# Attention block 1: normalizing the value products in place of the probabilities

## The chip, the cores and the metric

The kernel runs on one core of a Trainium2 chip. The metric is the device time of one launch in microseconds. The engines are TensorE (PE), VectorE (DVE), ScalarE (ACT), GpSimd (POOL) and the queue that issues transfers (SyncE, SP). They run side by side, each through its own list of instructions in order, and wait for one another by semaphores.

## The reference

Two transformer blocks on 256 positions of width 1024, in float32. The change is in the attention of the first one: 256 latent queries over 512 keys (256 of a context, 256 latent). Four A heads are differential: two softmaxes with 64-wide queries and keys, one minus lambda times the other, times 128-wide values, then an RMS norm over the 128 values. Eight B heads are ordinary, 96 wide, with 64-wide values.

```python
def _diff_attend(q1, q2, k1, k2, v, lam):
    s1 = einsum('bqhd,bkhd->bhqk', q1, k1) * scale
    s2 = einsum('bqhd,bkhd->bhqk', q2, k2) * scale
    a = softmax(s1) - lam * softmax(s2)
    return einsum('bhqk,bkhe->bqhe', a, v)

def _softmax_attend(q, k, v):
    a = softmax(einsum('bqhd,bkhd->bhqk', q, k) * scale)
    return einsum('bhqk,bkhe->bqhe', a, v)

oa = rmsnorm(oa, diff_subln) * (1 - lam_init)
out = concat(oa, ob) @ w_out
```

## The kernel before

Activations lie transposed: features on the 128 partitions, 256 positions along the row. Every weight matrix comes from memory in tiles of 128x2048 (`raw`, three buffers, issued by SP), and is split by ACT (`hi`) and DVE (`lo`) into two parts. Projections multiply these in three matmuls of 128x256 per 128x128 weight tile.

The program is first recorded, then ordered by a list scheduler written into the kernel (`schedule`, line 485): it has costs for each instruction, models the PE clock and the port that DVE and POOL share, takes for each engine the instruction that can start first (the order of the program breaks ties), and assigns buffers. Tiles of a tag (`tp`, `la`, `s`, ...) in PSUM are given out in the program's order. `BUFS` (line 683) gives `tp` two banks, `s` two, `la` and `v5` one each; scores alternate over `s`, `v5`, `s`. `issue` (line 635) then emits all instructions, so every row of the profile carries its line, L666, and rows are told apart by their tiles. There `c` stands for all 256- and 512-wide work tiles, `col` for columns, `v` for the tag `v5`.

Block 1's attention works on units: `unit` (line 1252) computes the softmax of one unit and then the value product of the unit before. A unit is one A head, or a pair of B heads.

- `softA` (line 1181): for each of two query tiles of 128 and each of the two softmaxes, a score matmul into PSUM, the maximum over 512 keys (DVE), its negated scaled copy (DVE), the exponential with the sum as a by-product (ACT). Then two reciprocals, lambda multiplied into the second, the second set of probabilities scaled (128x512; DVE for query tile 0, POOL for tile 1, `POOL_A`), and one DVE instruction that scales the first set and subtracts.
- `softB` (line 1220): the same with one softmax per query tile; the probabilities are scaled by 1 / z in a 128x512 instruction (POOL for query tile 0, DVE for tile 1, `POOL_B`).
- `transposed` (line 1162): eight PE transposes of 128x128 into two `tp` banks, each copied out by ACT (128x512).
- `pvA` (line 1204), `pvB2` (line 1239): value matmuls in full fp32 into the `la` bank, four of 128x256 for an A head, eight 64 wide for a B pair. A head's product is squared, its squares summed over the partitions by a matmul with ones, and normalized. The result is split into two parts in `cat`.

Between the units lie other pieces: the projections `qa`, `vc`, `kB`, `qB`, `vB` (`ORDER`); products of the `ada` matrices with a vector (`gemv`, line 975), whose 128x1024 multiplies go to DVE or POOL, in the latter case summed by ACT; and the output projection's terms for heads that are done (`wout_part`, line 1319).

Of the kernel before, what the change touches and what calls it, by code (L numbers as in the profile page):

```python
# [15 lines left out]
OP = mybir.AluOpType  # L16
# [662 lines left out]
def _build(ctx, tc, nc, A, out):  # L679
# [33 lines left out]
    def mm(o, a, b, start, stop):  # L713
        PE.matmul(o, a, b, start=start, stop=stop)
# [441 lines left out]
    V.tensor_tensor(lam[:, 2:3], lam[:, 0:1], lam[:, 1:2], OP.subtract)  # L1156
    lam_init = 0.8 - 0.6 * math.exp(-0.3 * 0)
    V.tensor_scalar(lam[:, 2:3], lam[:, 2:3], lam_init, None, op0=OP.add)
    subln = K("subln", [128, 1])
    V.tensor_scalar(subln, col("subln"), 1.0 - lam_init, None, op0=OP.mult)  # L1160

# [17 lines left out]
    SC = ("s", "v5", "s")  # L1179

    def softA(h):
        pa = []
        for qt in range(2):
            tq = slice(128 * qt, 128 * qt + 128)
            zs = T("col", [128, 2])
            pz = []
            for z in range(2):
                mx = T("col", [128, 2])
                r = slice(64 * z, 64 * z + 64)
                s_ = PSR([128, 512], SC)  # L1190
                mm(s_, qA[h][r, tq], kA[h][r], True, True)
                V.tensor_reduce(mx[:, 0:1], s_, AX.X, OP.max)
                V.tensor_scalar(mx[:, 1:2], mx[:, 0:1], -scA, None, op0=OP.mult)
                p = c2()
                ACT.activation(p, s_, AF.Exp, bias=mx[:, 1:2], scale=scA, accum_out=zs[:, z:z + 1])
                pz.append(p)
            V.reciprocal(zs, zs)
            V.tensor_tensor(zs[:, 1:2], zs[:, 1:2], lam[:, 2:3], OP.mult)
            (G if qt in POOL_A else V).tensor_scalar(pz[1], pz[1], zs[:, 1:2], None, op0=OP.mult)
            V.scalar_tensor_tensor(pz[0], pz[0], zs[:, 0:1], pz[1], op0=OP.mult, op1=OP.subtract)  # L1200
            pa.append(pz[0])
        return pa

    def pvA(h, pa):
        aT = transposed(pa)
        o_ = PS("la", [128, 256])
        for kt in range(4):
            mm(o_, vA[h // 2][kt][:, 128 * (h % 2):128 * (h % 2) + 128], aT[kt], kt == 0, kt == 3)
        sq = c1()
        ACT.activation(sq, o_, AF.Square)  # L1210
        st = PS("tp", [128, 256])
        mm(st, ones, sq, True, True)
        rs = c1()
        rstd_of(rs, st, 128)
        V.scalar_tensor_tensor(rs, o_, subln, rs, op0=OP.mult, op1=OP.mult)
        c_ = c2(F32R)
        split(c_[:, 0:256], c_[:, 256:512], rs)
        cat.append(c_)

    def softB(h):  # L1220
        pa = []
        for qt in range(2):
            tq = slice(128 * qt, 128 * qt + 128)
            mx = T("col", [128, 4])
            s_ = PSR([128, 512], SC)
            mm(s_, qB[h][0:96, tq], kB[h][0:96], True, True)
            V.tensor_reduce(mx[:, 0:1], s_, AX.X, OP.max)
            V.tensor_scalar(mx[:, 1:2], mx[:, 0:1], -scB, None, op0=OP.mult)
            p = c2()
            ACT.activation(p, s_, AF.Exp, bias=mx[:, 1:2], scale=scB, accum_out=mx[:, 2:3])  # L1230
            V.reciprocal(mx[:, 3:4], mx[:, 2:3])
            (G if qt in POOL_B else V).tensor_scalar(p, p, mx[:, 3:4], None, op0=OP.mult)
            pa.append(p)
        return pa

    def softB2(hp):
        return softB(2 * hp), softB(2 * hp + 1)

    def pvB2(hp, pas):
        o_ = PS("la", [128, 256])  # L1240
        aT = [transposed(pa) for pa in pas]
        for kt in range(4):
            for z in range(2):
                h = 2 * hp + z
                mm2(o_[64 * z:64 * z + 64], vB[kt][:, 64 * h:64 * h + 64], aT[z][kt], kt == 0, kt == 3)
        c_ = c2(F32R)
        split(c_[:, 0:256], c_[:, 256:512], o_)
        cat.append(c_)

    pend = []  # L1250
# [723 lines left out]
```

## Time and profile before

| | |
|---|---|
| median of 3 runs | 780.84 us (778.87 to 781.52) |
| the profiled execution | 778.39 us, of which the span from the first to the last instruction is 776.6 us |
| PE | 743.9 us busy (96%) |
| PE weight loads | 675.2 us (87%) |
| DVE | 583.5 us (75%) |
| ACT | 430.8 us (55%) |
| POOL | 304.9 us (39%) |
| mean granted PE clock | 0.995 of full speed |

Matmuls are pipelined, so that a matmul's duration is longer than the distance to the next one, and PE counts as busy over short gaps. The shares are means over the whole launch; the attention of block 1 takes the stretch from about 85 to 195 us.

### The profile page before, as it was taken

To read this page: it belongs to the slowest core of one execution; us is meant where nothing else is said; L and a number is where in the kernel's file an instruction comes from. 1 tells how busy PE (TensorE), PEld (TensorE's weight loads), DVE (VectorE), ACT (ScalarE), POOL (GpSimd) and SP (SyncE) were. 2 spreads that over 40 slices of the span, in tenths; PEclk is the share of its full clock that TensorE was granted. 3 is DMA by queue.
4 is the path that set the end of the run, shared out by engine and by line. 5 is a ranking of instruction groups with operands and counts; after the bars stand their busy time and mean duration, and the time that the engine had idled before them with its cause. 6 is when DMAs were issued, how large, how long until landed. Compare 5 with 4: busy or idle time off the path is not lost.

```text
span 776.6 us, 15213 instructions
## 1 busy us (share of the span) xinstructions
PE 743.9 (96%) x5987; PEld 675.2 (87%) x5987; DVE 583.5 (75%) x1106; ACT 430.8 (55%) x786; POOL 304.9 (39%) x313
## 2 busy tenths in 40 slices
PE   5998999999999999999999997899999999999998
PEld 3877785557999999999999996498899999999997
DVE  6768787977999899888668898976488666654552
ACT  6435439887765365555554432578556666643441
POOL 0013154764041949998012175686250333310000
PEclk9999899999999999999999999999999999999999
DMA  8956633434597366554666621053364655556540
GB/s 332 364 212 229 217 132 114 177 108 176 204 270 273 110 257 230 181 201 167 214 227 214 214 84 55 1 170 157 110 208 173 213 172 212 180 208 199 203 176 14
DMA packets 33993, 142.88 MB, mean 184 GB/s; under 512 B 11777, under 2 KB 15233, under 8 KB 17794
## 3 DMA queue, kind: packets, MB, share of 16 engines
q1 hardware_dynamic: 33922, 141.91, 51.7%
q8 instruction: 47, 0.77, 0.4%
q14 instruction: 24, 0.20, 0.1%
HBM read 139.54 MB, written 1.05 MB: 181 GB/s over the span
## 4 chain that ended last, share of the span: by engine, by line
PE 86%; DVE 8%; ACT 3%; DMA 1%; issue 1%; POOL 0%; SPq 0%; DVEq 0%
PE mm L666 42%; PE s L666 32%; PE tp L666 6%; DVE c L666 5%; PE la L666 4%; PE v L666 3%; ACT c L666 2%; DVE lo L666 1%; DVE col L666 1%; DMA raw<-in_ada 1%; DMA k_X<-in_x 0%; DVE raw L666 0%; DVE k_adc L666 0%; ACT raw L666 0%; ACT hi L666 0%
## 5 line engine op out<-in xcount | busy, mean ns | idle before, releaser
L666 DVE TENSOR_TENSOR lo<-raw,hi 128x1024 fp32r<-128x1024 f32 x206 | 263.0, 1280 | 82.3 <-ACT hi L666 81.0
L666 ACT ACTIVATE hi<-raw 128x1024 fp32r<-128x1024 f32 x206 | 216.2, 1053 | 193.1 <-PE mm L666 94.3
L666 PE MATMUL mm<-xs,hi 128*128 128x256 f32 (+1 forms) x992 | 179.6, 282 | 0.6 <-ACT hi L666 0.4
L666 PEld LDWEIGHTS mm<-xs,hi 128*128 128x128 f32 x992 | 151.4, 188 | 3.2 <-issue 1.4
L666 PE MATMUL mm<-c,hi 128*128 128x256 f32 (+1 forms) x744 | 141.8, 289 | 4.6 <-DVE c L666 2.7
L666 PE MATMUL mm<-xs,lo 128*128 128x256 f32 (+1 forms) x496 | 138.5, 280 | 2.0 <-DVE lo L666 2.0
L666 PEld LDWEIGHTS mm<-c,hi 128*128 128x128 f32 x744 | 115.1, 190 | 14.3 <-issue 4.7
L666 PE MATMUL s<-xs,hi 128*128 128x256 f32 (+1 forms) x672 | 123.0, 283 | 0.0
L666 PE MATMUL s<-c,hi 128*128 128x256 f32 (+1 forms) x676 | 120.2, 278 | 0.0
L666 PE MATMUL mm<-c,lo 128*128 128x256 f32 (+1 forms) x372 | 106.4, 287 | 1.2 <-DVE lo L666 1.2
L666 PEld LDWEIGHTS s<-c,hi 128*128 128x128 f32 x676 | 103.2, 188 | 1.4 <-issue 0.4
L666 PEld LDWEIGHTS s<-xs,hi 128*128 128x128 f32 x672 | 102.9, 188 | 0.7 <-issue 0.4
L666 PEld LDWEIGHTS mm<-xs,lo 128*128 128x128 f32 x496 | 93.8, 189 | 2.8 <-DVE lo L666 2.2
L666 PE MATMUL s<-xs,lo 128*128 128x258 f32 (+1 forms) x336 | 94.1, 280 | 2.2 <-DVE lo L666 2.2
L666 PE MATMUL s<-c,lo 128*128 128x256 f32 x338 | 94.2, 279 | 0.0
L666 ACT ACTIVATE c<-c 128x256 fp32r<-128x256 f32 (+4 forms) x141 | 61.7, 448 | 57.4 <-DVE c L666 54.4
L666 POOL TENSOR_TENSOR raw<-raw,k_crow 128x1024 f32<-128x1024 f32 x18 | 48.0, 2668 | 111.7 <-DMA raw<-in_ada 100.2
L666 DVE TENSOR_TENSOR c<-c,c 128x256 fp32r<-128x256 f32 (+2 forms) x115 | 65.0, 577 | 20.1 <-POOL c L666 15.7
L666 POOL TENSOR_TENSOR c<-c 128x256 f32<-128x256 f32 x40 | 41.7, 1042 | 89.2 <-ACT c L666 79.0
L666 PEld LDWEIGHTS mm<-c,lo 128*128 128x128 f32 x372 | 70.7, 191 | 3.0 <-DVE lo L666 1.6
L666 PEld LDWEIGHTS s<-xs,lo 128*128 128x128 f32 x336 | 63.8, 190 | 2.9 <-DVE lo L666 2.6
L666 PEld LDWEIGHTS s<-c,lo 128*128 128x128 f32 x338 | 63.5, 188 | 0.3
(251 smaller groups left out, 1119.4 us busy)
## 6 DMA issues: line engine op xcount, KB each, us to landing
raw<-in_wseq SPq DMA_DIRECT2D x102, 1024.0 KB, 4.8
raw<-in_ada SPq DMA_DIRECT2D x20, 1024.0 KB, 4.9
tab<-in_ada SPq DMA_DIRECT2D x4, 1024.0 KB, 7.4
c<-in_w SPq DMA_DIRECT2D x8, 256.0 KB, 4.6
k_X<-in_x SPq DMA_DIRECT2D x4, 256.0 KB, 4.8
raw<-in_wseq SPq DMA_DIRECT2D x2, 512.0 KB, 8.0
tab<-in_ctx SPq DMA_DIRECT2D x4, 256.0 KB, 10.6
out<-c SPq DMA_DIRECT2D x7, 128.0 KB, 2.4
```

The source lines that it names most:

```text
L666: getattr(self.real[o.eng], o.fn)(*[val(x) for x in o.args], **{k: val(x) for k, x in o.kw.items()})
```

## The change

The probabilities stay as the exponentials leave them. For A heads, with z0 and z1 the sums of the two softmaxes, the difference is formed as p0 - (lambda z0 / z1) p1 in one instruction, and the factor 1 / z0 of each query is left for the output. For B heads 1 / z is left for the output. Since queries lie along the row in the output, each 1 / z column is spread over the partitions: a matmul takes the column, broadcast to 128 (or 64) columns, as its stationary operand and the identity as the moving one, into a new `tp` tile, and ACT copies that to the work tile `rb`. The value product is multiplied by it (DVE, into `rb`), and what follows reads `rb`.

```diff
--- before.py
+++ after.py
@@ -1156,6 +1156,7 @@
     V.tensor_tensor(lam[:, 2:3], lam[:, 0:1], lam[:, 1:2], OP.subtract)
     lam_init = 0.8 - 0.6 * math.exp(-0.3 * 0)
     V.tensor_scalar(lam[:, 2:3], lam[:, 2:3], lam_init, None, op0=OP.add)
+    V.tensor_scalar(lam[:, 3:4], lam[:, 2:3], -1.0, None, op0=OP.mult)
     subln = K("subln", [128, 1])
     V.tensor_scalar(subln, col("subln"), 1.0 - lam_init, None, op0=OP.mult)
 
@@ -1179,10 +1180,10 @@
     SC = ("s", "v5", "s")
 
     def softA(h):
-        pa = []
+        pa, rz = [], T("col", [128, 2])
         for qt in range(2):
             tq = slice(128 * qt, 128 * qt + 128)
-            zs = T("col", [128, 2])
+            zs = T("col", [128, 4])
             pz = []
             for z in range(2):
                 mx = T("col", [128, 2])
@@ -1194,57 +1195,74 @@
                 p = c2()
                 ACT.activation(p, s_, AF.Exp, bias=mx[:, 1:2], scale=scA, accum_out=zs[:, z:z + 1])
                 pz.append(p)
-            V.reciprocal(zs, zs)
-            V.tensor_tensor(zs[:, 1:2], zs[:, 1:2], lam[:, 2:3], OP.mult)
-            (G if qt in POOL_A else V).tensor_scalar(pz[1], pz[1], zs[:, 1:2], None, op0=OP.mult)
-            V.scalar_tensor_tensor(pz[0], pz[0], zs[:, 0:1], pz[1], op0=OP.mult, op1=OP.subtract)
+
+            V.reciprocal(zs[:, 2:3], zs[:, 1:2])
+            V.reciprocal(rz[:, qt:qt + 1], zs[:, 0:1])
+            V.scalar_tensor_tensor(zs[:, 3:4], zs[:, 2:3], lam[:, 3:4], zs[:, 0:1], op0=OP.mult, op1=OP.mult)
+            V.scalar_tensor_tensor(pz[0], pz[1], zs[:, 3:4], pz[0], op0=OP.mult, op1=OP.add)
             pa.append(pz[0])
-        return pa
-
-    def pvA(h, pa):
+        return pa, rz
+
+    def pvA(h, pr):
+        pa, rz = pr
         aT = transposed(pa)
+
+        rr = PS("tp", [128, 256])
+        for qt in range(2):
+            mm2(rr[:, 128 * qt:128 * qt + 128], rz[:, qt:qt + 1].to_broadcast([128, 128]), ident, True, True)
+        rb = c1()
+        ACT.activation(rb, rr, AF.Copy)
         o_ = PS("la", [128, 256])
         for kt in range(4):
             mm(o_, vA[h // 2][kt][:, 128 * (h % 2):128 * (h % 2) + 128], aT[kt], kt == 0, kt == 3)
+        V.tensor_tensor(rb, o_, rb, OP.mult)
         sq = c1()
-        ACT.activation(sq, o_, AF.Square)
+        ACT.activation(sq, rb, AF.Square)
         st = PS("tp", [128, 256])
         mm(st, ones, sq, True, True)
         rs = c1()
         rstd_of(rs, st, 128)
-        V.scalar_tensor_tensor(rs, o_, subln, rs, op0=OP.mult, op1=OP.mult)
+        V.scalar_tensor_tensor(rs, rb, subln, rs, op0=OP.mult, op1=OP.mult)
         c_ = c2(F32R)
         split(c_[:, 0:256], c_[:, 256:512], rs)
         cat.append(c_)
 
     def softB(h):
         pa = []
+        rz = T("col", [128, 4])
         for qt in range(2):
             tq = slice(128 * qt, 128 * qt + 128)
-            mx = T("col", [128, 4])
+            mx = T("col", [128, 2])
             s_ = PSR([128, 512], SC)
             mm(s_, qB[h][0:96, tq], kB[h][0:96], True, True)
             V.tensor_reduce(mx[:, 0:1], s_, AX.X, OP.max)
             V.tensor_scalar(mx[:, 1:2], mx[:, 0:1], -scB, None, op0=OP.mult)
             p = c2()
-            ACT.activation(p, s_, AF.Exp, bias=mx[:, 1:2], scale=scB, accum_out=mx[:, 2:3])
-            V.reciprocal(mx[:, 3:4], mx[:, 2:3])
-            (G if qt in POOL_B else V).tensor_scalar(p, p, mx[:, 3:4], None, op0=OP.mult)
+            ACT.activation(p, s_, AF.Exp, bias=mx[:, 1:2], scale=scB, accum_out=rz[:, qt:qt + 1])
             pa.append(p)
-        return pa
+        V.reciprocal(rz[:, 2:4], rz[:, 0:2])
+        return pa, rz
 
     def softB2(hp):
         return softB(2 * hp), softB(2 * hp + 1)
 
     def pvB2(hp, pas):
         o_ = PS("la", [128, 256])
-        aT = [transposed(pa) for pa in pas]
+        aT = [transposed(pa) for pa, _ in pas]
+
+        rr = PS("tp", [128, 256])
+        for qt in range(2):
+            for z in range(2):
+                mm2(rr[64 * z:64 * z + 64, 128 * qt:128 * qt + 128], pas[z][1][:, 2 + qt:3 + qt].to_broadcast([128, 64]), ident, True, True)
+        rb = c1()
+        ACT.activation(rb, rr, AF.Copy)
         for kt in range(4):
             for z in range(2):
                 h = 2 * hp + z
                 mm2(o_[64 * z:64 * z + 64], vB[kt][:, 64 * h:64 * h + 64], aT[z][kt], kt == 0, kt == 3)
+        V.tensor_tensor(rb, o_, rb, OP.mult)
         c_ = c2(F32R)
-        split(c_[:, 0:256], c_[:, 256:512], o_)
+        split(c_[:, 0:256], c_[:, 256:512], rb)
         cat.append(c_)
 
     pend = []
```

## Rows read from the trace of the kernel before

**Rows 1.** Busy time of each engine in stretches (us, instructions in brackets), granted clock, DMA share
```profile
core 0: us, PE busy (x) PEld busy (x) DVE busy (x) ACT busy (x) POOL busy (x), PEclk, DMA share, GB/s
85.00:93.80 8.80, 7.54 (x27) 4.22 (x25) 5.56 (x11) 6.97 (x17) 0.00 (x0) 0.78 0.65 238
...
179.40:195.00 15.60, 15.56 (x123) 12.84 (x124) 11.86 (x16) 11.53 (x27) 5.34 (x3) 1.00 0.65 243
...
113.50:179.40 65.90, 60.28 (x288) 37.51 (x287) 52.54 (x125) 56.73 (x134) 39.54 (x22) 1.00 0.39 134
```

**Rows 2.** Chain that ended last, shares by engine and group, 113.5 to 179.4 us
```profile
by line: DVE c L666 22.6%; ACT c L666 15.3%; PE s L666 11.3%; DVE col L666 10.5%; PE la L666 10.0%; PE mm L666 6.4%; PE tp L666 5.5%; PE v L666 4.6%; DVE k_adc L666 3.3%; ACT raw L666 3.1%; DVE lo L666 2.6%; POOL c L666 2.4%; DVE raw L666 1
```

**Rows 3.** The same chain in order of time: start us, us, what
```profile
129.65 1.57 POOL c L666
...
131.24 2.86 DVE c L666
...
161.20 0.47 DVE c L666 x2
...
163.98 2.92 DVE c L666 x2
...
173.42 1.63 DVE c L666
```

**Rows 4.** ACT's groups, 113.5 to 179.4 us: busy us, mean ns, idle before, releasers
```profile
L666 ACT ACTIVATE c<-s,col 128x512 f32<-128x512 f32 x18 | 12.4, 692 | 4.2 <-DVE col L666 4.2
L666 ACT ACTIVATE c<-tp 128x512 f32<-128x512 f32 x18 | 10.2, 596 | 2.5 <-PE tp L666 2.4
...
L666 ACT ACTIVATE c<-c 128x256 fp32r<-128x256 f32 x4 | 1.7, 419 | 1.6 <-DVE c L666 1.6
...
L666 ACT ACTIVATE c<-la 128x256 fp32r<-128x256 f32 x2 | 0.8, 377 | 0.2 <-PE la L666 0.2
```

**Rows 5.** POOL's groups, 85 to 195 us
```profile
L666 POOL TENSOR_TENSOR raw<-raw,k_crow 128x1024 f32<-128x1024 f32 x12 | 30.0, 2508 | 11.8 <-DMA raw<-in_ada 11.8
L666 POOL TENSOR_SCALAR c<-c,col 128x512 f32<-128x512 f32 x12 | 20.5, 1712 | 18.6 <-PE la L666 9.2 <-DVE col L666 7.3 <-PE mm L666 2.0
```

**Rows 6.** DVE's groups, 85 to 195 us
```profile
L666 DVE TENSOR_SCALAR c<-c,col 128x512 f32<-128x512 f32 x12 | 13.1, 1102 | 0.1
...
L666 DVE TENSOR_TENSOR c<-la,c 128x256 fp32r<-128x256 f32 x4 | 1.7, 415 | 0.5 <-ACT c L666 0.5
```

**Rows 7.** Instructions on the one-column tiles (col): count, ns min/median/max, first and last start
```profile
L666 DVE TENSOR_REDUCE col<-s x21: 662/680/692, 86.9 to 175.8; 128x1 f32<-128x512 f32 x21
...
L666 DVE TENSOR_SCALAR c<-c,col x12: 472/487/2662, 97.5 to 182.6; 128x512 f32<-128x512 f32 x12
...
L666 DVE SCALAR_TENSOR_TENSOR c<-c,col,c x8: 729/750/2857, 98.3 to 152.4; 128x512 f32<-128x512 f32 x8
```

**Rows 8.** POOL's instructions in order of time: start us, us
```profile
99.36 1.59 POOL L666 TENSOR_SCALAR c<-c,col 128x512 f32<-128x512 f32 x1 [0.80 <-DVE col L666]
...
164.26 2.35 POOL L666 TENSOR_TENSOR raw<-raw,k_crow 128x1024 f32<-128x1024 f32 x1 [4.07 <-DMA raw<-in_ada]
```

**Rows 9.** DVE's instructions in order of time
```profile
100.34 1.22 DVE L666 TENSOR_TENSOR lo<-raw,hi 128x1024 fp32r<-128x1024 f32 x1
...
164.24 2.66 DVE L666 TENSOR_SCALAR c<-c,col 128x512 f32<-128x512 f32 x1
```

**Rows 10.** ACT's instructions in order of time
```profile
167.00 0.69 ACT L666 ACTIVATE c<-s,col 128x512 f32<-128x512 f32 x1 [2.08 <-DVE col L666]
...
175.88 0.69 ACT L666 ACTIVATE c<-s,col 128x512 f32<-128x512 f32 x1 [1.00 <-DVE col L666]
```

**Rows 11.** The chain's PE pieces: two value products and a set of transposes
```profile
156.01 1.73 PE la L666 x8
...
182.75 1.88 PE la L666 x16
...
185.30 0.87 PE tp L666 x8
```

## The prediction

> **What bounds the kernel now.** I read the table of stretches first, to find the stage the edit touches and what its engines have to spare [rows 1]. The reader is to see three stretches. Between 85 and 93.8 us the granted clock averages 0.78 of full speed: part of it runs at the lower level, 1.2 GHz. From 113.5 to 179.4 us comes most of the softmax and value work of the eight units of heads (four A heads, four pairs of B heads); the clock is full, ACT is busy 56.7 us of 65.9, DVE 52.5, POOL 39.5. From 179.4 us on PE is busy 15.56 us of 15.60: the output projection fills it, and the rest of the kernel follows without a gap.
>
> Then the chain that ended last, for the middle stretch [rows 2]. DVE rows hold the largest shares (DVE c 22.6%, DVE col 10.5%), ACT c 15.3%; the PE groups listed sum to 37.8%. So most of this stage is latency of the softmax, and time saved here reaches the end, since PE's dense work behind it only waits to start. Before 113.5 us the first A head runs beside the qa and vc projections; there I expect nothing.
>
> The chain in order of time [rows 3] shows single pieces that belong to the scaling: a POOL scaling (1.57 us at 129.65), the DVE subtraction behind it that took 2.86 us, and DVE scalings at 161.20 (0.47), 163.98 (2.92) and 173.42 (1.63). ACT's groups [rows 4] show 4.2 us of idle before the exponentials that wait for DVE's maxima, and 2.5 us before the copies of transposed probabilities. POOL and DVE groups [rows 5, 6] give the scaling's totals.
>
> **What is removed.** Twelve POOL scalings, 20.5 us busy [rows 5], and twelve DVE scalings, 13.1 us [rows 6]. An undisturbed one on DVE takes 0.49 us (the median), the longest 2.66 [rows 7]; so 13.1 - 12 x 0.49 = 7.2 us of DVE's total is time blocked. What blocks it is seen in the instructions in order of time: the scaling at 164.24 ran 2.66 us beside the POOL multiply of an ada matrix at 164.26, which took 2.35 [rows 8, 9]. These multiplies stay (12 of them, 30.0 us [rows 5]), so the blocking goes only with the blocked operation. The maxima queued behind that scaling, for which ACT waited 2.08 us, read one PSUM tile, and no such reduction took more than 0.69 us [rows 7], so they should now run early; the same wait was 1.00 us at 175.88 [rows 10].
>
> On the chain the removed pieces are 1.57 (POOL), 0.47, 2.92 - 0.42 = 2.5 (a split subtraction of about 0.42 us shares that piece) and 1.63, and the excess of the subtraction at 131.24 over its median, 2.86 - 0.75 = 2.1 [rows 3, 7]. Sum 8.3 us. The last is unsure: the subtraction stays, and can be blocked by a multiply elsewhere.
>
> **What is added.** Small DVE columns: A gets one more one-column instruction per query tile (8), B loses one per head (8); they cancel.
>
> DVE: one 128x256 multiply with one PSUM operand in each of 8 units; its nearest row is the split's subtraction, 0.42 us [rows 6]: 3.3 us in all. B's four split subtractions now read two SBUF operands, so a POOL multiply can block them, up to 2.66 us; what waits for them is only the output projection, which has other heads' terms to do. I take nothing, and keep one such block in the range.
>
> ACT: one 128x256 copy from PSUM per unit at 0.38 us [rows 4], 3.0 us; B's split copies and A's squares now read SBUF, 0.42 instead of 0.38 [rows 4], 0.3 us more. Six units (A0 to A3, B0, B1) end within the middle stretch: 6 x 0.38 + 0.2 = 2.5 us there.
>
> PE: the trace has no full fp32 matmul of a broadcast column with 128 columns. A head's four value matmuls of 256 columns appear as eight instructions in 1.73 us, 0.216 each; a pair's eight matmuls, 64 wide, as sixteen in 1.88 us, 0.118 each [rows 11]. Half the columns, half the time: A 2 x 2 x 0.108 = 0.43 us, B 4 x 2 x 0.059 = 0.47 us. Lower end: one pass, like eight transposes in 0.87 us [rows 11], so 0.22 and 0.22 (two abreast); upper end: no time saved by the shorter stream, 0.87 and 0.94. I take the halved value, since the length halved is the only difference to the nearest row. In the middle stretch PE waits anyway. B2 and B3 end in the dense stretch, where nothing covers it: 2 x 0.47 = 0.9 us on the path (0.4 to 1.9).
>
> The two-bank tag for transposes takes one more tile per unit, held until ACT's copy, so the value matmuls get a copy and the results a multiply more of latency. In return, A's single value bank comes free after one multiply, not after the norm; I price that at nothing to 1 us and take nothing.
>
> **The sum, reckoned twice.** By the chain: if none of the additions lies on it, -8.3 + 0.9 = -7.4 us; if all lie on it for six units, each 0.43 (PE) + 0.38 (ACT) + 0.42 (DVE) = 1.23, +7.4: 0.0. Middle -3.7. By ACT, which is 86% busy and takes the chain over when DVE is relieved: idle before exponentials 4.2 us goes, of the 2.5 us before transposed copies half (they wait for scaled probabilities, but for PE too), so -5.4 + 2.5 + 0.9 = -2.0 us. Both limits act at once, so I take the mean, -2.8 us. The profiled execution took 778.39 us (span 776.6, the rest around it): 775.6. The three runs shown have a median 2.45 us above it, 780.84; from that, **778.0 us**. A measurement of this kernel can tell about 0.3% from no change, 2.3 us; the forecast lies just beyond.
>
> **Against the Trainium skill.** During the POOL scaling at 99.36 (1.59 us) DVE subtracted two SBUF operands at 100.34 in 1.22 us, undisturbed; only the two-operand multiplies of POOL show DVE instructions stretched to their end [rows 8, 9]. The Trainium skill, "SBUF — State Buffer", section "Who interferes with whom", says otherwise: a DVE instruction with two SBUF inputs, or in a two-port mode, shares an exclusive lock with any GpSimd instruction that reads SBUF, and the second fully blocks. By that rule the twelve POOL scalings block DVE as well, their removal gives more, and the sum would be that of the first rival below, -5.8 us, in place of -2.8 by the rows. The rows here don't bear the rule out for the scaling, and do for the multiply; I go by them.
>
> **Rivals.**
> *Deeper relief (chance 0.13).* DVE is freed not only of its own scalings but of hindrance by the 20.5 us of POOL scalings [rows 5], and ACT runs without gaps. ACT's idle in the middle stretch, 65.9 - 56.7 = 9.2 us, is the ceiling: -9.2 + 2.5 + 0.9 = -5.8 us, 775.0. For: DVE's 7.2 us of blocking. Against: ACT also waits for PE, and the subtraction at 100.34. This is what the rule of "SBUF — State Buffer" in the Trainium skill would bring.
> *Hidden (0.31).* Only the waits at 167.00 and 175.88 go (3.1 us), and ACT's 2.5 and PE's 0.9 return: +0.3 us; with half a us to two more from the transposes, about -1: 779.8, within 0.3%. For: from 125 to 143 us ACT is already almost always busy. Against: the DVE pieces on the chain.
> *ACT becomes the bound, slower (0.17).* The exponentials wait for PE's scores as before, and each added copy delays the next exponential: 3.3 us of ACT and 0.9 of PE uncovered, with one of ACT's waits saved: +4.2 - 1.0 = +3.2 us, 784.0. It decides if less than about 1 us of ACT's 9.2 us idle disappears.
> *Another order, slower (0.05).* The scheduler in the kernel orders all engines anew; a stall like that at 85 us could put PE at 1.2 GHz once more. There 8.8 us at 0.78 lost 8.8 x 0.22 = 1.9 us and PE idled 8.80 - 7.54 = 1.3 [rows 1]: +3.2 us, 784.0.
> That the scaling isn't removed cannot be: the code has none left.
>
> **Chances.** The forecast itself (2.4 to 5 us faster) gets 0.34. Faster by over 0.3%: 0.34 + 0.13 = 0.47; within: 0.31; slower: 0.17 + 0.05 = 0.22. Range, 772.5 to 784: below, the chain with nothing added back (-7.4, 773.4) and up to 1 us from the value bank; above, the two slower cases. The forecast's own range is 775.5 to 779.
>
> **What would show it.** In the changed profile: no POOL or DVE 128x512 scaling from 85 to 190 us, POOL down by about 20 us, DVE by about 10 (13.1 less 3.3), ACT up by about 3; idle before the exponentials well under 4.2 us; the start of PE's dense stretch some 3.7 us earlier than 179.4 (2.8 and the 0.9 that it gives back); the new matmuls at about 0.1 us an instruction. I am wrong if ACT's waits for DVE return at other places (multiplies of POOL that block the subtractions of A or weight splits in front of maxima), if transposes wait for their bank, or if weights arrive too late for the earlier dense stretch.

## The result, and the profile after

The changed kernel is slower, by 0.8%: 784.72 us in the median of 12 runs (781.44 to 790.82), against 778.68 us of 12 runs of the kernel before; the ratio is 1.0079, with a 95% interval of 1.006 to 1.0099. The profiled execution has a span of 783.5 us; that of the kernel before had 776.6.

The scalings are gone, as the groups of the changed kernel from 85 to 195 us show (busy us, mean ns, idle before, releasers):

```profile
L666 POOL TENSOR_TENSOR raw<-raw,k_crow 128x1024 f32<-128x1024 f32 x12 | 31.2, 2607 | 28.5 <-DMA raw<-in_ada 27.8 <-ACT c L666 0.8
...
L666 DVE SCALAR_TENSOR_TENSOR c<-c,k_subln,c 128x256 f32<-128x256 f32 x4 | 5.3, 1328 | 0.0
...
L666 DVE TENSOR_TENSOR c<-la,c 128x256 f32<-128x256 f32 x8 | 3.4, 423 | 9.0 <-PE la L666 8.9
...
L666 ACT ACTIVATE c<-tp 128x256 f32<-128x256 f32 x8 | 3.2, 401 | 1.4 <-PE tp L666 1.4
...
L666 PE MATMUL tp<-k_cst,col 128*64 128x128 f32 x32 | 2.8, 284 | 0.0
...
L666 PE MATMUL tp<-k_cst,col 128*128 128x128 f32 x16 | 2.7, 294 | 3.9 <-ACT c L666 3.9
```

No scaling on POOL or DVE is left, where [rows 5, 6] had twelve each. The additions are there as well: eight DVE multiplies of 0.42 us, eight ACT copies of 0.40, and 48 PE instructions for the spreading, 5.5 us busy (durations of matmuls that follow one another overlap). The ACT groups of the middle stretch answer to [rows 4]:

```profile
L666 ACT ACTIVATE c<-s,col 128x512 f32<-128x512 f32 x15 | 10.5, 701 | 1.3 <-DVE col L666 1.2
L666 ACT ACTIVATE c<-tp 128x512 f32<-128x512 f32 x16 | 9.1, 603 | 0.5 <-PE tp L666 0.5
```

The waits that the scalings caused shrank as forecast: 4.2 us to 1.3 before these exponentials, 2.5 to 0.5 before the copies (for 15 and 16 instructions in the stretch, where it held 18 of each). So the relief took place. But part of ACT's waiting for DVE came back elsewhere. All of it in the middle stretch (us in total, times, longest), in the kernel before and then in the changed one:

```profile
ACT c L666 <- DVE col L666: 4.2, 4, 2.1
...
ACT c L666 <- DVE c L666: 2.0, 3, 1.3
```

```profile
ACT c L666 <- DVE c L666: 2.9, 4, 1.6
ACT c L666 <- DVE col L666: 2.2, 2, 1.2
```

That is 5.1 us in place of 6.2. The stretches of the changed kernel, in the columns of [rows 1], tell why the relief is worth so little:

```profile
core 0: us, PE busy (x) PEld busy (x) DVE busy (x) ACT busy (x) POOL busy (x), PEclk, DMA share, GB/s
113.50:179.40 65.90, 61.24 (x325) 41.19 (x326) 47.88 (x112) 58.38 (x140) 25.19 (x13) 1.00 0.41 142
179.40:195.00 15.60, 15.60 (x125) 12.29 (x124) 7.92 (x17) 10.64 (x25) 0.00 (x0) 1.00 0.56 202
```

In the middle stretch DVE has 4.7 us less to do and POOL 14.4 us less, but PE is busy 61.24 us of 65.90, and was busy 60.28 before [rows 1]. PE had 5.6 us to give in this stretch, and has 4.7 now. The chain that ended last says the same. Its shares from 113.5 to 179.4 us, and some of its pieces in order of time (start us, us, what):

```profile
by line: PE mm L666 19.5%; PE la L666 16.6%; PE tp L666 16.1%; PE s L666 15.3%; DVE c L666 11.8%; PE v L666 8.8%; ACT c L666 7.4%; issue 2.7%; DVE col L666 2.0%
...
124.54 2.39 DVE c L666 x2
...
127.09 1.27 ACT c L666 x3
...
137.00 2.62 DVE c L666 x2
...
152.86 0.45 PE tp L666 x4
...
162.95 0.59 PE tp L666 x8
...
167.82 2.33 DVE c L666
```

The PE groups sum to 76.3%, against 37.8% in [rows 2]. PE's last wait ends, and its dense stretch starts, at 171.63 us instead of 179.4, almost eight us earlier, yet the residual update behind it comes at the same time, 196.46 us against 196.56: the work that PE did beside the DVE chain before now stands in a row, with the spreading matmuls in it (0.45 us of an A head at 152.86, 0.59 of a B pair at 162.95).

Three DVE pieces are left on the chain, and they are no scalings. The instructions of the changed kernel in order of time, DVE's and then POOL's (start us, us, and what each is):

```profile
124.54 2.06 DVE L666 SCALAR_TENSOR_TENSOR c<-c,k_subln,c 128x256 f32<-128x256 f32 x1
...
137.00 2.29 DVE L666 SCALAR_TENSOR_TENSOR c<-c,k_subln,c 128x256 f32<-128x256 f32 x1
...
167.82 2.33 DVE L666 TENSOR_TENSOR c<-c,c 128x256 fp32r<-128x256 f32 x1
...
123.93 2.39 POOL L666 TENSOR_TENSOR raw<-raw,k_crow 128x1024 f32<-128x1024 f32 x1
...
136.62 2.39 POOL L666 TENSOR_TENSOR raw<-raw,k_crow 128x1024 f32<-128x1024 f32 x1
...
164.61 7.77 POOL L666 TENSOR_TENSOR raw<-raw,k_crow 128x1024 f32<-128x1024 f32 x3 [1.23 <-DMA raw<-in_ada]
```

Each runs beside a POOL multiply of an ada matrix. The first two end 0.28 us after it (at 126.60 and 139.29 us, the multiplies at 126.32 and 139.01), as the scaling at 164.24 did in [rows 8, 9]; the third lies within a row of three multiplies. The norm of an A head read its product from PSUM and took 0.46 to 0.48 us in the kernel before, as here:

```profile
149.05 0.47 DVE L666 SCALAR_TENSOR_TENSOR c<-la,k_subln,c 128x256 f32<-128x256 f32 x1
```

Now that the product lies in the work tile `rb`, this instruction reads two SBUF operands and takes 1.33 us in the mean. The Trainium skill, "SBUF — State Buffer", section "Who interferes with whom", has DVE instructions with two SBUF inputs contend with GpSimd instructions that read SBUF. For the multiplies the trace agrees (2.06 to 2.33 us instead of 0.42 to 0.48).

PE pays for these three blocks. From 113.5 us to the residual update it waits three times, each time for ACT's work behind one of them (the wait stands in brackets):

```profile
128.41 0.71 PE L666 MATMUL tp<-k_cst,col 128*128 128x128 f32 x4 [1.17 <-ACT c L666]
...
141.10 0.71 PE L666 MATMUL tp<-k_cst,col 128*128 128x128 f32 x4 [2.78 <-ACT c L666]
...
171.63 0.66 PE L666 MATMUL tp<-k_cst,c 128*128 128x128 f32 x4 [0.69 <-ACT c L666]
```

The sum is 4.64 us, all but 0.02 of PE's idle time in the middle stretch. So the waits that the scalings made went, and others came in their place.

So the attention doesn't gain. Where does the loss come from? First the stretches of the kernel before that [rows 1] don't have, up to the residual update at 196.56 us and in two later stages (columns as above):

```profile
85.00:100.00 15.00, 13.74 (x68) 10.42 (x67) 10.27 (x26) 9.44 (x22) 1.53 (x2) 0.77 0.55 205
100.00:196.56 96.56, 90.43 (x522) 63.37 (x522) 77.79 (x152) 71.29 (x167) 52.95 (x28) 1.00 0.43 151
...
265.00:280.00 15.00, 15.00 (x128) 14.94 (x127) 14.76 (x20) 7.54 (x12) 14.61 (x12) 1.00 0.39 141
475.00:500.00 25.00, 19.55 (x135) 13.26 (x136) 23.09 (x106) 9.26 (x40) 15.55 (x24) 1.00 0.13 43
```

The same of the changed kernel, and its first 20 us:

```profile
0.00:20.00 20.00, 10.91 (x55) 6.24 (x56) 13.17 (x77) 11.84 (x19) 1.45 (x7) 0.91 0.91 327
85.00:100.00 15.00, 13.74 (x93) 11.26 (x92) 13.06 (x35) 9.51 (x23) 1.92 (x3) 1.00 0.65 232
100.00:196.46 96.46, 91.35 (x553) 65.62 (x553) 68.86 (x144) 74.49 (x176) 33.16 (x15) 1.00 0.46 162
265.00:280.00 15.00, 12.42 (x90) 12.01 (x89) 12.57 (x18) 4.01 (x7) 14.61 (x12) 0.89 0.41 141
475.00:500.00 25.00, 20.85 (x162) 16.19 (x163) 19.46 (x83) 8.17 (x33) 11.33 (x17) 0.80 0.13 43
```

Up to the residual update four amounts add up to the -0.1 us. The changed execution was 1.7 us late at the first scores (its clock was 0.91 in the first 20 us). The kernel before lost 15 x (1 - 0.77) = 3.45 us to the clock from 85 to 100 us, the changed one nothing. PE's idle time fell from 6.13 to 5.11 us. What is left, -0.1 - 1.7 + 3.45 + 1.0 = 2.6 us, is put down to added PE work. So the attention itself costs some 1.6 us, which the better clock of this one execution hides. The rest comes later, in code that the diff doesn't touch: 3.2 us by 405 us, 6.9 at 536 us and from there to the end. There the changed execution shows PE idle 2.58 us from 265 to 280 us where it wasn't before, and granted clocks of 0.89 and 0.80 where it was 1.00 before.

### The profile page after: what moved, and what is told of

Same layout as the page of the kernel before. It is cut to its first block, busy times and chain, and to the rows that moved or that the text cites. A ratio compares the mean times of both kernels' runs of the same rounds, so it can differ in the third digit from the quotient of the medians.

```text
span 783.5 us, 15286 instructions
## 1 busy us (share of the span) xinstructions
PE 751.2 (96%) x6035; PEld 682.6 (87%) x6035; DVE 571.5 (73%) x1103; ACT 434.5 (55%) x794; POOL 285.5 (36%) x301
## 4 chain that ended last, share of the span: by engine, by line
PE 89%; DVE 6%; DMA 2%; ACT 1%; issue 1%; SPq 0%; POOL 0%; DVEq 0%; POOLq 0%
PE mm L666 43%; PE s L666 32%; PE tp L666 7%; PE la L666 4%; DVE c L666 4%; PE v L666 3%; DVE lo L666 1%; DMA raw<-in_wseq 1%; ACT c L666 1%; DMA raw<-in_ada 1%; DVE col L666 0%; DVE raw L666 0%; SPq L666 0%; ACT hi L666 0%; POOL k_crow L666 0%
## 5 line engine op out<-in xcount | busy, mean ns | idle before, releaser
L666 PE MATMUL mm<-xs,hi 128*128 128x256 f32 (+1 forms) x992 | 181.7, 284 | 0.2 <-ACT c L666 0.2
L666 PEld LDWEIGHTS mm<-xs,hi 128*128 128x128 f32 x992 | 153.7, 191 | 2.5 <-issue 1.4
L666 PE MATMUL mm<-xs,lo 128*128 128x256 f32 (+1 forms) x496 | 140.2, 283 | 2.5 <-DVE lo L666 2.5
L666 ACT ACTIVATE c<-c 128x256 fp32r<-128x256 f32 (+4 forms) x149 | 65.2, 448 | 60.6 <-DVE c L666 57.5
L666 DVE TENSOR_TENSOR c<-c,c 128x256 fp32r<-128x256 f32 (+2 forms) x119 | 67.8, 579 | 18.8 <-POOL c L666 15.7
```

Source lines behind the costliest of these rows:

```text
L666: getattr(self.real[o.eng], o.fn)(*[val(x) for x in o.args], **{k: val(x) for k, x in o.kw.items()})
```

## The experiments

The diff's edit was taken apart in two ways. The scheduler draws the order of all engines in one go, so a change in the attention also changes the order of all later work. In most experiments the later order is pinned: for every instruction recorded after the attention (from the residual update on) the kernel first plans another variant, and each engine then takes these instructions in that plan's order. The order within the attention is not pinned (but for part of it in e3): each variant of the attention brings its own.

```diff
+            if PLAN:
+                plan = record(sp, pp, nc, A, out, PLAN)
+                plan.prepare()
+                for i in plan.schedule():
+                    o = plan.ops[i]
+                    if o.key and (PIN == "all" or o.key[1]):
+                        rec.pin.setdefault(o.eng, []).append(o.key)
...
-                for pr, i in sorted(h)[:60]:
+                q = self.pin.get(e, ())
+                for pr, i in [x for x in sorted(h)[:60] if ops[x[1]].key not in self.pinned or ops[x[1]].key == q[0]]:
```

The runs of one kernel scatter by up to 1.5%, in step with the granted clock: over 295 runs of all kernels, one slope for all, 0.01 of mean clock goes with 6.0 us of span. The last column moves each kernel's mean span to full clock with that slope (standard error 0.1 to 0.5 us; the kernel before 773.1 in 117 runs: 773.4 beside e1 to e4, 772.8 beside e5 to e8, 773.1 beside e9 to e12, 773.3 beside e13 to e15). It parts work and order from the falls of the clock; differences below about 0.8 us between two variants are within its error.

| kernel | median us | before, us | ratio, 95% interval | at full clock, us |
|---|---|---|---|---|
| changed | 784.72 | 778.68 | 1.0079 [1.006, 1.0099] | 777.7 |
| e1 new attention, old late order | 782.01 | 779.19 | 1.0027 [0.9997, 1.0056] | 775.3 |
| e2 old attention, new late order | 782.51 | 779.19 | 1.0036 [1.0013, 1.006] | 775.6 |
| e3 new attention, all else in old order | 787.81 | 779.19 | 1.0098 [1.0061, 1.0135] | 781.0 |
| e4 as e1, product kept in PSUM | 783.69 | 779.19 | 1.0059 [1.0033, 1.0086] | 777.7 |
| e5 as e1, no spreading on PE | 779.37 | 778.75 | 1.0020 [0.9995, 1.0045] | 773.6 |
| e6 A heads folded, B old, old late order | 777.95 | 778.75 | 0.9996 [0.9971, 1.0021] | 772.7 |
| e7 A heads as changed, B old | 781.12 | 778.75 | 1.0019 [0.9995, 1.0042] | 773.4 |
| e8 B heads as changed, A old | 778.72 | 778.75 | 1.0010 [0.9981, 1.004] | 774.0 |
| e9 before, late order drawn anew (+2%) | 787.32 | 778.43 | 1.0107 [1.0073, 1.0141] | 777.0 |
| e10 before, late order drawn anew (-2%) | 784.46 | 778.43 | 1.0054 [1.0024, 1.0084] | 775.5 |
| e11 as e6, spreading in one pass | 775.63 | 778.43 | 0.9976 [0.9945, 1.0007] | 770.8 |
| e12 as e1, spreading done twice | 782.83 | 778.43 | 1.0051 [1.0025, 1.0077] | 777.6 |
| e13 the kernel of e11 again | 776.91 | 777.84 | 0.9982 [0.9958, 1.0006] | 771.0 |
| e14 as e11, all orders free | 781.15 | 777.84 | 1.0033 [1.0007, 1.0059] | 774.0 |
| e15 changed, late order drawn anew | 788.56 | 777.84 | 1.0129 [1.0083, 1.0175] | 779.3 |

### Attention or order: e1 to e4

**e1**: the changed attention, the later instructions pinned to the order of the kernel before (`RUN, PLAN, PIN = "AB", "-", "late"`).

> The changed attention, but everything recorded after it (from the residual update on) is put on each engine in the order that the scheduler gave it in the kernel before. In the two profiles the first feed-forward result comes at 212.8 us before and 212.7 us after, and the 6.9 us of the longer span build up behind that point (3.2 us by the end of the first feed-forward, 6.9 us by the gated linear unit). Theory of the order (the loss is made by the new order of unchanged work): within about 1.5 us of the kernel before, 0 to -2 likelier than a loss. Rival, the stage itself (attention's own new work costs the time and the later delay is only its consequence): 5 us or more slower, like the changed kernel. Rival, the clock (stalls that were there already now meet a fall of the granted clock by their timing): somewhere between, with the falls at other places than in the changed kernel's profile.

**e2**: the old attention, the later instructions in the order of the changed kernel (`"-", "AB", "late"`).

> The attention of the kernel before, with its scalings, but everything recorded after it in the order that the scheduler gave it in the changed kernel. Theory of the order: 4 to 7 us slower than the kernel before, though not one instruction is new. The stage itself: within 1.5 us of the kernel before.

**e3**: as e1, and the work between the units of attention pinned to its old order too (`PIN = "all"`).

> The changed attention, and all other instructions, those interleaved with the attention too (projections, weight splits, products of the ada matrices, transfers), in the order of the kernel before; only the attention's own instructions are placed freely between them. Theory of the order: 0 to 3 us faster than the kernel before, since the scalings are gone and nothing else moved. The stage itself: slower by 2 us or more, since the order of before was made for the scalings.

**e4**: as e1, with the product left in PSUM:

```diff
-        V.tensor_tensor(rb, o_, rb, OP.mult)
+        V.tensor_tensor(o_, o_, rb, OP.mult)
+        rb = o_
```

> As e1, but the product of value result and 1/z is written in place into the la bank, and what follows reads it there, as before the change. In the changed profile the norm's last instruction of two A heads takes 2.06 and 2.29 us where it took 0.47 before, and two split subtractions take 1.95 and 2.33 us, each beside a POOL multiply: they now read two operands from SBUF. If that blocking costs time: 1.5 to 4 us faster than e1, and no such instruction over 0.6 us. If it is hidden: within 1 us of e1.

The loss divides in two, and neither theory has it all. The attention alone costs 775.3 - 773.1 = 2.2 us at full clock, the later order alone 2.5; together 4.7, and the changed kernel lies 4.6 above the kernel before. (e1's interval for itself just includes no change. Counted from the kernel before that ran beside them, the two are 2.0 and 2.2.) In e1 the clock from 85 to 100 us is the same as before, so its stretches compare directly:

```profile
85.00:100.00 15.00, 13.74 (x68) 10.43 (x67) 10.35 (x28) 9.46 (x21) 0.75 (x1) 0.77 0.53 201
100.00:197.62 97.62, 92.50 (x564) 67.00 (x564) 66.56 (x147) 74.28 (x175) 34.91 (x16) 1.00 0.46 160
```

PE is busy 2.07 us longer than in the kernel before (92.50 against 90.43) and idle 1.01 us less (5.12 against 6.13): 1.06 us later at the residual update, and this with DVE 11 us less busy. That is half of the 2 us; where the other half comes about, behind the residual update and with the old order held, was not looked into.

e3 is the slowest of the four: with the work between the units held in its old order too, the time is 7.9 us longer at full clock, 5.7 more than in e1, from which only this order differs. So an order within the attention can cost more than the whole edit; e3 says nothing on the later order alone. e4 came out as neither of its expectations, slower than e1. It took the second SBUF operand from the norm and the splits, and a block then met another instruction that reads two SBUF operands, as its instructions in order of time show, DVE's and then POOL's:

```profile
162.06 1.68 DVE L683 TENSOR_TENSOR c<-c,c 128x256 fp32r<-128x256 f32 x1
...
163.72 3.31 DVE L683 TENSOR_TENSOR lo<-raw,hi 128x1024 fp32r<-128x1024 f32 x1
...
158.65 10.62 POOL L683 TENSOR_TENSOR raw<-raw,k_crow 128x1024 f32<-128x1024 f32 x4 [16.93 <-DMA raw<-in_ada]
```

A weight split took 3.31 us beside four POOL multiplies in a row, and PE idled 6.0 us from 100 us to the residual update. That e4 is 2.4 us worse than e1 may come from the single value bank, held until the norm; no run tested that.

### Which part of the attention: e5 to e8

**e5**: as e1, without the spreading matmuls.

```diff
-        rr = PS("tp", [128, 256])
...
-        ACT.activation(rb, rr, AF.Copy)
+        ACT.activation(rb, aT[0], AF.Copy)
```

> The new attention with the order of e1, without the matmuls that spread 1 / z: ACT copies a tile of transposed probabilities in place of the spread factors, and the value product is multiplied by that, so the factors 1 / z are left out; ACT and DVE do as much as in e1. Theory that PE is the bound of the whole attention stage: in e1 the spreading matmuls took 5.4 us of PE's busy time from 85 to 200 us, and the chain from 113 to 198 us was almost all PE; without them the attention gives back 3 to 5 us, and the time is about 778 us, 4 us under e1 (782.0) and 1 us under the kernel before (779.2). Rival, blocked DVE instructions: the chain of e1 holds three pieces of 2.3 to 2.6 us of DVE instructions beside POOL multiplies, which stay: 781 to 783 us. Rival, ACT's added copies: these stay too: 781 to 783 us.

**e6**: only the A heads, with z0 taken out by the norm.

```diff
-            V.reciprocal(rz[:, qt:qt + 1], zs[:, 0:1])
+            V.scalar_tensor_tensor(rz[:, qt:qt + 1], zs[:, 0:1], 128 * EPS, zs[:, 0:1], op0=OP.mult, op1=OP.mult)
...
-        mm(st, ones, sq, True, True)
+        mm2(st, ones, sq, True, False)
+        for qt in range(2):
+            mm2(st[:, 128 * qt:128 * qt + 128], rz[:, qt:qt + 1].to_broadcast([128, 128]), ident, False, True)
```

> Only the A heads are changed, and in another way: the value product keeps its factor z0, and the norm takes it out, since the mean square of the scaled product plus epsilon equals (mean square + epsilon z0 squared) / z0 squared. So only epsilon z0 squared is spread by the matmuls, added into the norm's sum in PSUM; there is no ACT copy and no DVE multiply, and the norm's last instruction reads PSUM as in the kernel before. B heads and the late order as before. Theory that PE is the bound: four units of spreading remain, about 2.7 us of PE, against the gain from the A heads' scalings; near the kernel before, 778.5 to 781 us. Theory of the blocked DVE instructions: the two blocks of the A heads' norm that stand in the chain of e1 are gone, and the A heads' scalings with them: 775 to 777.5 us.

**e7** and **e8**: one kind of head as in the changed kernel, the other as before (`RUN = "A"`, `"B"`).

> The A heads as in the changed kernel, the B heads and the late order as before. PE is the bound: half of e1's loss, 780 to 781.5 us. Blocked DVE instructions: two of the three blocks in the chain of e1 belong to the A heads' norm, so most of the loss or more, 782 to 784 us. Latency and banks (the extra tile for transposes): about half, as PE.

> The B heads as in the changed kernel, the A heads and the late order as before. PE is the bound: half of e1's loss, 780 to 781.5 us. Blocked DVE instructions: one block of three, against eight scalings on DVE and eight on POOL that go: 778 to 780 us.

e5 came out between the theories: 779.37 us, where PE's theory had 778 and its rivals 781 to 783. At full clock it is 1.7 us faster than e1 (773.6 against 775.3), or 1.2 if each is counted from the kernel before that ran beside it (0.8 above 772.8, 2.0 above 773.4). So the spreading matmuls carry more than half of e1's loss; but without them the attention is only back near the kernel before. The copies, the multiplies and the blocks were left, and PE idled 6.1 us from 100 us to the residual update (95.82 - 89.70), as much as before: the relief of the scalings by itself, with these left, gained PE nothing. Counted in the same way the A heads alone lose 0.6 us (e7) and the B heads alone 1.3 (e8), each with an error of about 0.35. The theory of the blocked instructions wanted most of the loss with the A heads, and the runs speak against that; half and half, as PE's theory wanted, is within the error.

e6 came out between its two expectations as well, 777.95 us, and by its ratio at the kernel before. There the norm reads PSUM again and the copies and multiplies are gone; PE's idle time fell to 2.7 us (98.94 - 96.22). So what PE waited for can be removed, but with four units of spreading the time stays the same. Whether the spreading is what takes the gain, the next runs ask.

### The dose on PE: e11 to e13

**e11**: as e6, with the spreading in fp32r.

```diff
+        rz = T("col", [128, 2], F32R)
+        identr = K("identr", [128, 128], F32R)
...
-            mm2(st[:, 128 * qt:128 * qt + 128], rz[:, qt:qt + 1].to_broadcast([128, 128]), ident, False, True)
+            mm2(st[:, 128 * qt:128 * qt + 128], rz[:, qt:qt + 1].to_broadcast([128, 128]), identr, False, True)
```

> As e6 (A heads changed, the factor folded into the norm's epsilon, B heads and late order as before), with the spreading matmuls in fp32r, one pass in place of two. Theory that PE is the bound of the stage: in e6 PE's idle time from 100 us to the residual update fell to 2.7 us from 6.1, and the four units of spreading took about as much back; with half of that gone, about 1 us faster than e6, 776.5 to 777.5 us. Rival, that the stage's time hangs on DVE and ACT: as e6, 778 us.

**e12**: as e1, each spreading matmul issued twice.

```diff
-        for qt in range(2):
+        for qt in (0, 1, 0, 1):
```

> e1 with every spreading matmul done twice (the second overwrites the first with the same values). Theory that PE is the bound: again what the first set cost, 1 to 2.7 us over e1 (0.27% over the kernel before): 0.4% to 0.65% over the kernel before, 782 to 784.5 us. Rival, that PE has idle time to hide it: as e1.

**e13**: e11 again.

> The kernel of e11 once more, since its interval (0.9945 to 1.0007) just reaches one. If PE's relief in the attention is real: 0.25% to 0.4% faster than the kernel before. If e11's median was a lucky draw of the clock: within 0.1%.

Doubled, the spreading costs 2.3 us more at full clock (777.6 against 775.3), 0.29 us for each of the eight units; leaving it out had saved 1.2 to 1.7. PE has no time to hide it, as its theory wanted. With the cheaper spreading the A heads' part turns into a gain: e11 and e13 have ratios of 0.9976 and 0.9982. Their mean is 0.9979, with a half width of sqrt(0.0031^2 + 0.0024^2) / 2 = 0.0020: faster than the kernel before by 0.2%, with the bound of the interval at nothing; at full clock 2.2 us. e11 and e13 are 1.9 and 1.7 us faster than e6, from which they differ in half of the spreading of four units; at 0.29 us a unit that would be 0.6 us. The rest may lie in the order within the attention, which e11 has drawn anew as well; no run parts the two. The stretches of e11:

```profile
85.00:100.00 15.00, 13.74 (x94) 11.26 (x93) 13.06 (x33) 10.07 (x22) 3.56 (x3) 1.00 0.58 209
100.00:191.52 91.52, 88.59 (x505) 61.96 (x505) 68.17 (x151) 70.31 (x166) 45.49 (x23) 1.00 0.46 162
...
475.00:500.00 25.00, 21.68 (x119) 14.82 (x118) 19.32 (x98) 9.36 (x40) 16.03 (x25) 0.80 0.00 1
```

The residual update comes at 191.52 us, 5.04 before that of the kernel before. Of this 3.45 us is the clock from 85 to 100 us, which stayed full; PE's idle time is 2.93 us instead of 6.13, a gain of 3.2, and the remaining 1.6 (88.59 - 90.43 + 3.45) is PE's added work, with what moved across the ends of the stretch.

The stage can be read from one profile of each variant in the same way, from the first score matmul to the residual update, less the time that the granted clock withheld. It takes 107.4 us in the kernel before, and 107.4 to 107.8 with the old attention in e2, e9 and e10. With the new one it takes 107.9 us without the spreading (e5), 108.6 with it (e1) and 110.5 with it doubled (e12). With the A heads alone folded it takes 106.5 (e6), 105.7 (e11) and 104.9 (e13). So within each group more work on PE goes with a longer stage, by smaller steps than in the times at full clock. One kind of head alone takes 107.6 (e7) and 107.1 us (e8), which does not add up to e1's 1.2.

### Any new order: e9, e10, e14, e15

**e9** and **e10**: the kernel before, with another cost of DVE in the scheduler for the later instructions alone (1.02 and 0.98).

```diff
+        if self.late and eng == "V":
+            o.dur *= 1.02
```

> The computation of the kernel before, all of it, with the old attention; only the scheduler's cost of a DVE instruction is 2% higher for everything recorded after the attention (from the residual update on), so that only the order of the later work is drawn again. Theory that any new order of the later work costs what e2 showed, because the order of the kernel before is a good one of many: 1 to 4 us slower than the kernel before. Rival, that e2's order is bad for a reason that lies in the changed attention (its later or earlier end): no difference, within 1 us.

> As e9, with the cost 2% lower. The same two theories: 1 to 4 us slower than the kernel before, or within 1 us of it. If one of the two is slower and the other not, the cost of an order is scattered, and e2's 2 to 3 us is a draw from that scatter.

**e14**: e11 with nothing pinned. **e15**: the changed kernel with the edit of e9.

> The attention of e11, with all orders left to the scheduler. Theory that a new order of the later work costs 2 us and more whatever the attention: 0.1% to 0.8% slower than the kernel before, 2 to 8 us slower than e11. Rival, that the changed kernel's later order is bad for what its attention does: as e11.

> The changed kernel, with the scheduler's cost of a DVE instruction 2% higher for everything recorded after the attention. Theory that the order is a draw: another time than the changed kernel's (0.79% over the kernel before), by 1 us or more to either side, and still over the kernel before, since its attention alone costs 0.27% (e1).

A new order of the later work costs 2.4 to 3.9 us at full clock with the old attention, untouched (e2, e9, e10), 3.0 to 3.2 with that of e11 (e14 against e13 and e11), though e14's attention stage, 104.1 us, is no longer than theirs; and the changed kernel drawn once more is another 1.6 us slower. (By medians, falls of the clock included, e9 and e10 are 8.9 and 6.0 us slower, more than the 1 to 4 that were expected.) All five new orders are worse than the one that the kernel before has. Part of what differs is seen in PE's waits for weight splits (`lo`) from 213 to 345 us (us in total, times, longest), in the kernel before, the changed kernel and e9:

```profile
PE s L666 <- DVE lo L666: 2.2, 2, 1.2
```

```profile
PE s L666 <- DVE lo L666: 3.3, 2, 2.1
```

```profile
PE s L685 <- DVE lo L685: 6.0, 2, 4.1
```

The same row has 2.5 us in e10, 4.3 in e14 and 3.9 in e15, and 2.2 in e11, which keeps the old order. PE waits for a weight split that stands in DVE's queue behind other pieces. In e9 it is seen around the longest wait, in order of time, DVE's instructions and then POOL's and PE's:

```profile
277.66 2.27 DVE L685 SCALAR_TENSOR_TENSOR c<-c,c 128x256 f32<-128x256 f32 x1
...
281.18 4.01 DVE L685 TENSOR_TENSOR lo<-raw,hi 128x1024 fp32r<-128x1024 f32 x3
...
276.30 3.35 POOL L685 TENSOR_TENSOR raw<-raw,k_crow 128x1024 f32<-128x1024 f32 x1
...
282.97 0.58 PE L685 MATMUL s<-xs,lo 128*128 128x258 f32 x1 [4.11 <-DVE lo L685]
```

The instruction at 277.66 takes 2.27 us beside a POOL multiply (one of the same kind at 284.93 us in the changed kernel, with none beside it, takes 0.47), the split comes after it, and PE stands still for 4.11 us. The clock then adds its part: e9's mean granted clock over its runs is 0.986 against 0.993 of the kernel before beside it, which by the slope is about 4.5 us.

## Why the prediction was wrong

The forecast was 778.0 us, 2.8 faster; it came out 784.72 and lies above the range (772.5 to 784). The forecast counted from 780.84 us, the median of the three runs shown; twelve runs of the kernel before have 778.68, so the loss is 6.0 us where a gain of 2.8 was forecast.

**What is removed and added: right.** DVE's busy time fell from 583.5 to 571.5 us (forecast about -10), POOL's from 304.9 to 285.5 (-20), ACT's rose from 430.8 to 434.5 (+3). The multiplies took 0.42 us, the copies 0.40. The new matmuls took about 0.1 us an instruction, as forecast. The waits at the scalings fell, and PE's dense stretch starts earlier by even more than forecast, 7.8 us instead of 3.7.

**The sum: wrong, at "in the middle stretch PE waits anyway" and at the blocks that it took at nothing.** These are the steps that failed in the attention. The sum looked for the engine that takes over after DVE, and took ACT, 86% busy. PE stood in the same row of [rows 1] with 60.28 of 65.90 us, 91%. Its idle 5.6 us was the ceiling of any gain in that stretch as long as PE's own work stays, and the first reckoning, with up to 7.4 us, lies above it. The spreading had to be paid from the same idle time. The reckoning by ACT lets PE's work of six units vanish and puts 0.9 us on the path; that by the chain covers half of it. Measured, PE does 2.1 us more in e1 and idles only 1.0 less.

That so little of the idle time went is the other half. The sum had -5.4 us for ACT's waits and took nothing for two-operand instructions that a POOL multiply blocks, B's splits. The norm of the A heads, which comes to read two SBUF operands as well, it did not count at all. Three such blocks, two of the norm and one of a split, stand on the changed kernel's chain, and PE's 4.64 us of waits follow them. It is the prediction's own sign of being wrong, that ACT's waits for DVE return at other places, and it came true. Where the norm reads PSUM and the copies and multiplies are gone too (e6 and e11, with the B heads as before), PE idles 2.7 and 2.9 us from 100 us to the residual update, in place of 6.1. No run takes the blocks alone away: e4 tried, other blocks came, and the time grew.

The price of one spreading was not the error: 0.43 and 0.47 us were forecast, and the pieces of the chain have 0.45 and 0.59, the doubling 0.29.

**The chance of another order: wrong.** The rival had the mechanism, all engines ordered anew, with a stall and a fall of the clock, and gave it 0.05 and a place beside the attention. The runs put most of it behind the attention, in code that the diff leaves as it is, and e9, e10, e14 and e15 show that it came with every new plan that was tried. Its price, 2.5 us at full clock in e2, was near the 3.2 forecast. It is not a rival to the rest but is added to each of the cases; that was not seen.

**The rivals.** "ACT becomes the bound" named the right kind of case, an engine that is full taking the added work uncovered, with the wrong engine; that its 784.0 us lies near the measured 784.72 is luck, since 2.5 us of the loss come from the later order. "Deeper relief" has nothing for it: even with no spreading on PE (e5) the attention is no faster than before, though all twelve POOL scalings are gone. The prediction has this rival's 5.8 us as what the rule of the Trainium skill ("SBUF — State Buffer", "Who interferes with whom") would bring; no run here tests the rule for the scaling by itself.

**What stays open.** The full-clock numbers explain 4.6 of the 6.0 us between the medians; of the other 1.4, about 1.1 goes by the slope with the mean granted clock, 0.991 of the changed kernel against 0.993. How much the time scatters with the order within the attention was not measured: e3 shows 5.7 us for one such order, while the effects read from e1, e5, e6 and e11 are about 2 us. So that PE's fullness decides the attention is borne out by the doubling and by the stage times, and not free of this rival. Why every new order drawn here is worse than that of the kernel before is shown only for one stage (PE's waits for splits); the stretch from 440 to 540 us, where the profiled executions part by another 3.7 us, was not taken apart; the clock from 475 to 500 us alone is 25 x 0.20 = 5.0 us there.

## What to carry to other kernels

Before pricing relief of the engines on the chain, take the idle time of every other engine in that stretch: the smallest is the ceiling of the gain, and work that the change adds to that engine is paid from it first, so that a change that moves work from less busy engines (DVE, POOL) to the fullest one (PE) can lose even where it shortens the chain. List every instruction that comes to read its operands from another place, since such a one may be blocked where the removed one was. Where one scheduler orders the whole program, a local edit also redraws all that follows; hold that order fixed to see what the edit is worth, and redraw it alone to see what a draw costs. Here the edit cost about 2 us, the draw 2.5, and the version with the fewest additions (e11: no copy, no multiply, spreading in one pass) gained 2.2 us only while the old order was held.

## What was not expected of the hardware

The clock falls after the same wait in one execution and not in another. PE idles 1.16 us near 89 us in the kernel before, in e1 and in e11 (at 88.8, 88.7 and 88.8 us); the granted clock from 85 to 100 us is 0.77 in the first two and 1.00 in the third. Nor does a difference of the clock need another kernel: e13 is e11 again, and from 475 to 500 us it has

```profile
475.00:500.00 25.00, 21.20 (x126) 13.00 (x127) 22.05 (x109) 10.64 (x43) 18.40 (x27) 0.95 0.05 21
```

0.95, where e11 had 0.80, and a span of 773.4 us instead of 775.9. So a stall's cost in one profile, here several us, is not the cost in the median, and differences of a few us between two profiled executions have to be cleared of the clock first.
